# A decoder layer on one core: the operands that TensorE streams are put 64 bytes off the ones it keeps, and the MLP gets a fifth weight buffer

## Chip, cores and metric

One NeuronCore of a Trainium2 chip runs the whole layer as one program. The metric is the device time of one execution in microseconds; the time before is the median of 3 runs. TensorE (PE in the profile) multiplies, VectorE (DVE) and ScalarE (ACT) prepare operands and do the element-wise work, SyncE (SP) issues the DMAs that bring weights from HBM to SBUF. PEld is TensorE's loading of the operand that it keeps.

## What is computed

One layer over 16 meta tokens and 256 real tokens with model width 2048, in float32:

```
u = rmsnorm(h, g_mix);  proj = u @ w_in            # 2048 x 6144, q/k/v of both head groups
o_diff = rmsnorm(differential attention, 8 heads)  # softmax(q1 k1) - lam * softmax(q2 k2)
o_sb = rmsnorm(stick-breaking attention, 8 heads)
h = h + concat(o_diff, o_sb) @ w_out               # 2048 x 2048
m = rmsnorm(h, g_mlp)
h = h + square(relu(m @ w_up)) @ w_down            # 2048 x 8192 x 2048
return h without the meta tokens
```

## The kernel before

**Products in three.** Every float32 operand of a large matmul is kept as two tiles of TensorE's rounded float32 type: `hi`, a rounded copy made by ACT, and `lo`, the rest, made by DVE (`split`, lines 168 to 173). A product is then three matmuls: hi by hi, hi by lo and lo by hi. Each matmul has an operand that TensorE keeps (`lhsT`, 128 columns, loaded ahead) and one that it streams (`rhs`, 256, 272 or 512 columns).

**Parts.** Weights arrive by DMA in blocks of 128 x 1024 (`raw`, five buffers) and are split into a *part*: a `whi` and a `wlo` tile. There are 96 parts of `w_in`, 32 of `w_out` (numbers 96 to 127 here) and, from `first_mlp` on (number 128), those of the MLP. Three part buffers serve the first two stages. The MLP has four (`MLP_PARTS`): the fourth, tag "v", holds each part whose number counted from 128 leaves 3 when divided by 4. A part is prepared up to `MLP_LEAD` parts ahead of the one that TensorE uses, and a buffer is free again once the part `MLP_PARTS` back has been used (`ring`).

**Three stages.** (1) `w_in`, up to about 340 us: `products` (lines 944 to 956) keeps a block of weights and streams a row of `u`, 272 columns wide; for two of the six kinds of strips (`a in (0, 3)`, the queries) the first 16 columns, the meta tokens, are left out and 256 are streamed. Attention of finished heads is woven in between. (2) `w_out`, up to about 434 us: `triple` keeps `mixed` and streams 512 columns of weights. (3) The MLP in 8 rounds of 1024 hidden columns: `triple2` keeps `w_up` and streams 256 columns of `m` (line 1038), and `triple` keeps `hid` and streams `w_down` (line 1044). In three of the four column groups of rounds 0 to 6, and one in round 7 (`FAST`), a 2 x 2 block product is done with seven block products in place of eight; its seven weight blocks come from one load as part "a" (split of 768 columns, then three sums on DVE, lines 267 to 272, that turn `raw` into four further blocks) and part "b" (split of those). "b" can only be split once the sums of "a" are there. The other column groups are done plainly, 512 columns at a time.

**Order.** All instructions are recorded in a fixed order by a planner (`Pace`), which has a time estimate of its own for each engine and lets a job (a split, an evacuation) go into the queues when its inputs are due. On the chip each engine works through its queue strictly in that order. The evacuation of an up strip (`up_evac`, lines 841 to 870) makes `hx` and `hid` on ACT and DVE; the latter is what the down products of the next round keep.

**Where things lie.** The addresses in a partition are fixed when the program is built. Taken modulo 128 bytes: `u` (and `m`, in the same place), `mixed`, the `hid` of even rounds and the three part buffers all start at 32; the `hid` of odd rounds (a tile of its own) and the fourth part buffer start at 96. Parts, `m`, `mixed` and `hid` have rows of 1024 bytes or multiples of 512, so each block in them keeps its tile's remainder. A row of `u` has 272 columns, 1088 bytes, which is 8 x 128 + 64: its `hi` rows stand at 32 and its `lo` rows at 96. Where the 16 meta columns are left out, 64 bytes are added. The text below calls the start of the kept operand minus the start of the streamed one, modulo 128, the **offset** of a matmul. Before, it is 0 or 64 in all large matmuls:

| matmuls | streamed columns | count | offset before |
|---|---|---|---|
| up | 256 | 3072 | 0 in 2640 (110 parts), 64 in 432 (18 parts in the fourth buffer) |
| down, seven products | 256 | 1848 | 0 in 921, 64 in 927: even rounds 0 (fourth buffer 64), odd rounds 64 (fourth buffer 0) |
| down, plain | 512 | 480 | 0 in 240, 64 in 240 |
| out | 512 | 384 | 0 |
| in, keys and values | 272 | 1536 | in turn 0, 64, 0 within each product |
| in, queries | 256 | 768 | in turn 64, 0, 64 within each product |

The last 16 KB that the change uses come from a scratch area for DMA descriptors at the bottom of each partition, 16,384 bytes before (`dynamic_dma_scratch_size` at its default); the kernel issues all its DMAs from SP.

Of the kernel before, what the change touches and what calls it, by code (L numbers as in the profile page):

```python
# [7 lines left out]
F32 = mybir.dt.float32  # L8
F32R = mybir.dt.float32r
AF = mybir.ActivationFunctionType  # L10
ALU = mybir.AluOpType
AX = mybir.AxisListType

P = 128
DM = 2048
SEQ = 256
META = 16
TOK = META + SEQ
KT = DM // P
EPS = 1e-6  # L20
NEG = -1e30
ROUNDS = 8
PAIRS = 4
RAW = 5
# [1 line left out]
KINDS = ((0, 3, 1, 2, 4, 5), (1, 0, 2, 4, 3, 5), (1, 0, 2, 4, 3, 5), (1, 0, 4, 3, 2, 5))  # L26
PARTS = 3
LEAD = 2
MLP_PARTS = 4
MLP_LEAD = 3  # L30
FAST = {(r, u) for r in range(ROUNDS - 1) for u in range(3)} | {(ROUNDS - 1, 0)}
PSUM_BANKS = {"acc": 4, "att": 4}
SLOTS = {"k": 4, "q": 4, "v": 2, "e": 3, "pr": 2, "ah": 2, "m": 2, "n": 2}
# [86 lines left out]
def hymba_layer(ctx: ExitStack, tc: tile.TileContext, xT_d, xh_d, win_d, wout_d, wup_d, wdn_d, cst_d, par_d, out_d):  # L120
    nc = tc.nc
    cp = ctx.enter_context(tc.tile_pool(name="const", bufs=1))
    big = ctx.enter_context(tc.tile_pool(name="big", bufs=1))
    wp = ctx.enter_context(tc.tile_pool(name="weights", bufs=1))
# [10 lines left out]
    def as32(ap):  # L135
        return ap.bitcast(F32)
# [18 lines left out]
    cst = tp.tile([P, C_ID], F32, bufs=1, name="cst")  # L155
    ident = cp.tile([P, P], F32, name="ident")
    xT = big.tile([P, KT, TOK], F32, tag="x", name="xT")
    um = big.tile([P, KT, 2, TOK], F32R, tag="act", name="u")
    mixed = big.tile([P, KT, 2, SEQ], F32R, tag="mix", name="mixed")

    def split_u(k):
        g = par[:, G_MIX + k : G_MIX + k + 1]
        nc.scalar.activation(um[:, k, 0, :], xT[:, k, :], AF.Copy, scale=g)
        nc.vector.scalar_tensor_tensor(
            um[:, k, 1, :], xT[:, k, :], g, as32(um[:, k, 0, :]), op0=ALU.mult, op1=ALU.subtract
        )

    def split(hi, lo, src, n):
# [7 lines left out]
    strips = []  # L176
# [9 lines left out]
    order = [("in", *u) for u in dict.fromkeys(u[:2] for u in units)]  # L186
# [3 lines left out]
    def up(r, i, cs):  # L190
        return [("up", r, i, c) for c in cs if r < ROUNDS]

    def down(r, u, ps):
        return [(x, r, u, p) for p in ps for x in ("ab" if (r, u) in FAST else "a")]

    order += up(0, 0, range(3)) + up(0, 1, range(3)) + up(0, 0, (3,)) + up(0, 1, (3,)) + up(0, 2, range(4)) + up(0, 3, range(4))
    for r in range(ROUNDS - 1):
        c = iter([key for i in range(PAIRS) for key in up(r + 1, i, range(4))])
# [4 lines left out]
        assert not [*c, *d]  # L203
    ab = iter(down(ROUNDS - 1, 0, range(PAIRS)))
    d = iter([key for u in (1, 2, 3) for key in down(ROUNDS - 1, u, range(PAIRS))])
    order += [next({"d": d, "a": ab, "b": ab}[x]) for x in "dd" + "adbd" * 4 + "dd"]
# [5 lines left out]
    def source(g):  # L212
        what, *at = order[g]
        if what == "in":
            (_, a, b), c = strips[at[0]], at[1]
            return win_d[a, b][:, 4 * c : 4 * c + 4]
        return {"out": wout_d, "up": wup_d, "a": wdn_d}[what][tuple(at)]

    raws, parts, raw_at, done_at, parted = {}, {}, {}, {}, set()
    dma = [1700.0]  # L220

    def load(dst, src, n):
        nc.sync.dma_start(dst, src)
        dma[0] = max(dma[0], pc.pe + 1700) + n * 1.42
        return dma[0] + 400

    def fetch(number, pieces=1):
        if number < len(loads):
            g = loads[number]
            raws[g] = wp.tile([P, 4, 256], F32, tag="raw", bufs=RAW, name=f"raw_{g}")  # L230
            n = 4 // pieces
            for i in range(pieces):
                k = slice(n * i, n * i + n)
                raw_at[g, i] = load(raws[g][:, k], source(g)[:, k], n * 256)
                yield
# [3 lines left out]
    def part(g, pieces=1):  # L239
        if g < len(order) and g not in parts:  # L240
            pool, bufs, tag = wp, PARTS, "w"
            if g >= first_mlp:
                ring[g] = max(g - MLP_PARTS, first_mlp - PARTS + (g - first_mlp) % MLP_PARTS) if (g - first_mlp) % MLP_PARTS < PARTS else g - MLP_PARTS
                if (g - first_mlp) % MLP_PARTS >= PARTS:
                    pool, bufs, tag = mp, MLP_PARTS - PARTS, "v"
                    ring[g] = ring[g] if g - MLP_PARTS >= first_mlp else -1
            hi = pool.tile([P, 4, 256], F32R, tag=tag + "hi", bufs=bufs, name=f"whi_{g}")
            lo = pool.tile([P, 4, 256], F32R, tag=tag + "lo", bufs=bufs, name=f"wlo_{g}")
            parts[g] = (hi, lo)
            what, *at = order[g]  # L250
            fast = what in "ab" and (at[0], at[1]) in FAST
            pc.job("weights", (fast_a if what == "a" else fast_b)(g, hi, lo) if fast else halves(g, hi, lo, pieces))
# [31 lines left out]
    def halves(g, hi, lo, pieces):  # L284
        n = 4 // pieces
        for i in range(pieces):
            src = (g, i) if (g, i) in raw_at else (g, 0)
            while src not in raw_at or ring[g] >= 0 and ring[g] not in done_at:
                yield pc.pe + 200, None
            yield max(raw_at[src], done_at.get(ring[g], 0.0)), "a"  # L290
            k = slice(n * i, n * i + n)
            t = yield from split(hi[:, k], lo[:, k], raws[g][:, k], 256 * n)
            for kk in range(n * i, n * i + n):
                pc.at["w", g, kk] = t
        parted.add(g)
# [3 lines left out]
    g = 0  # L299
    for c in range(4):  # L300
        n = 2 if c == 0 else 4
        w = fetch(g, 4 // n) if g < RAW else None
# [473 lines left out]
    m = H = mp = None  # L776
# [52 lines left out]
    def mtile(tag, shape, name, bufs=1, dt=F32):  # L829
        return mp.tile(shape, dt, tag=tag, bufs=bufs, name=name)  # L830
# [2 lines left out]
    hid, Z = {}, {}  # L833

    def hidden(r):
        if r % 2:
            hid[r] = mtile("hid", [P, PAIRS, FULL, 2, P], f"hid_{r}", 1, F32R)
        else:
            hid[r] = big.tile([P, PAIRS, FULL, 2, P], F32R, tag="mix", name=f"hid_{r}")
# [32 lines left out]
    def plain_evac(r, u, o):  # L872
        yield from pc.until("R2")
        yield pc.pe, "v"
        for i in range(2):
# [3 lines left out]
            pc.give("acc", t)  # L879
            if r == ROUNDS - 1:  # L880
                nc.sync.dma_start(out_d[:, u, i], H[:, u, i])
# [86 lines left out]
    def later(number):  # L968
        while number < len(loads) and loads[number - RAW] not in parted:
            yield pc.pe + 200, None  # L970
        yield from ((pc.pe, None) for _ in fetch(number))
# [20 lines left out]
    for g in range(LEAD + 1):  # L992
        part(g, 2)
# [8 lines left out]
    def begin(g, lead):  # L1002

        if g:
            for later_g in range(g + 1, g + lead + 1):
                if later_g <= g + LEAD or later_g >= first_mlp:
                    part(later_g, 2 if later_g < 6 else 1)
        if g in load_of:
            pc.job("fetch", later(load_of[g] + LEAD + RAW))

    for s, c, kks in units:
        g = index["in", s, c]
# [6 lines left out]
        hi, lo = parts[g]  # L1019
        for j in range(2):  # L1020
            for kk in kks:
                k = 4 * c + kk
# [27 lines left out]
    for g in range(index["out", 0, 0], first_mlp):  # L1050
        _, u, c = order[g]
        if c == 0:
            out = banks("acc", 2, f"out_{u}")
            if u == 0:
                m = big.tile([P, KT, 2, SEQ], F32R, tag="act", name="m")
        if u == 1 and c == 0:
            while pc.lanes["head"][0] or any(("mixed", k) not in pc.at for k in range(KT)):
                pc.pe += 100
                pc.pump()
            attention.close()  # L1060
            mp = ctx.enter_context(tc.tile_pool(name="mlp", bufs=1))
        begin(g, LEAD)
        hi, lo = (x.rearrange("p (k a) b -> p k (a b)", k=2) for x in parts[g])
        for kk in range(2):
            k = 2 * c + kk
            pc.stall(("w", g, 2 * kk + 1), ("mixed", k))
            for i in range(2):
                x = [mixed[:, k, a, P * i : P * i + P] for a in range(2)]
                t = triple(out[i], x, (hi[:, kk], lo[:, kk]), k == 0, k == KT - 1)
                pc.pump()  # L1070
        done_at[g] = pc.pe
        if c == 7:
            pc.job("evac", after(t, out_evac(u, out)))
            if u == 3:
                pc.job("once", mlp_norm())

    for g in range(first_mlp, len(order)):
        what, r, u, p = order[g]
        begin(g, MLP_LEAD)
        hi, lo = parts[g]  # L1080
        pc.stall(("w", g, 3))
        if what == "up":
# [3 lines left out]
            for j in range(2):  # L1086
                for kk in range(4):
                    k = 2 * p + kk % 2 + 8 * (kk // 2)
                    pc.stall(("m", k))
                    w = [x[:, kk, P * j : P * j + P] for x in (hi, lo)]  # L1090
# [4 lines left out]
        else:  # L1095
            fast = (r, u) in FAST
            pc.stall(("hid", r, p))
            x = lambda slot: [hid[r][:, p, slot, a] for a in range(2)]
# [15 lines left out]
            else:  # L1114
                for i in range(2):
                    for k in range(2):
                        w = [y[:, 2 * k : 2 * k + 2].rearrange("p a b -> p (a b)") for y in (hi, lo)]
# [8 lines left out]
def _tables():  # L1126
# [12 lines left out]
    q, k = np.arange(P)[:, None], np.arange(P)[None, :]  # L1139
    cst[:, C_MD : C_MD + P] = np.where(k <= q, 0.0, NEG)  # L1140
    strict = np.where(k < q, 0.0, NEG)
    cst[:, C_MS + K0 : C_MS + TOK] = strict
# [44 lines left out]
```

## Time and profile before

| | |
|---|---|
| median of 3 runs | 1145.86 us (1145.79 to 1147.93) |
| the profiled execution | 1145.84 us, of which the span of instructions is 1144.0 us |
| busy: PE, PEld, DVE, ACT | 1131.5, 1082.5, 950.1, 799.2 us |
| granted clock of TensorE | 1.000 |
| HBM read | 206.49 MB |

Matmuls overlap in the records (each lasts about 0.28 us, and the next starts about 0.12 us after it), so that PE's busy time says little: its pace is read from the starts. In the chain of waits, a piece "PE up L1038 x24" is a run of 24 matmuls on the path that ends last, with its length in us ahead of it.

### The profile page before, as it was taken

The numbers are of one execution on the slowest core, as the hardware profiler recorded it, in microseconds if no ns is written. First come the engines' busy times: TensorE is split into PE (matmuls) and PEld (weight loads), VectorE is DVE, ScalarE is ACT, GpSimd is POOL, SyncE is SP. The second block draws the span as 40 slices with busy tenths as digits, with TensorE's granted clock in tenths as the row PEclk, the third lists the DMA queues.
The fourth block names the chain that finished last, engine by engine and source line by source line (L and its number), as shares of the span: only waits on it lengthen the run. The fifth ranks groups of instructions, "written<-read, shape, count | busy, mean of one in ns | idle before, by whom it ended". The sixth has DMA issues, their size and how long they took to land.

```text
span 1144.0 us, 21838 instructions
## 1 busy us (share of the span) xinstructions
PE 1131.5 (99%) x8599; PEld 1082.5 (95%) x8599; DVE 950.1 (83%) x1459; ACT 799.2 (70%) x1283; POOL 1.1 (0%) x8
## 2 busy tenths in 40 slices
PE   9999999999999999999999999999999999999998
PEld 7999999999998889999999999999999999999987
DVE  6987987887976556788888898898888888888997
ACT  7769888778776545666677676677677677677763
POOL 0000000000000000000000000000000000000000
PEclk9999999999999999999999999999999999999999
DMA  8564544555545556556555555555555655565554
GB/s 328 185 221 138 158 133 148 155 157 156 160 147 168 184 184 201 166 185 197 197 193 189 184 195 190 183 192 193 192 186 187 203 198 186 189 198 187 186 184 163
DMA packets 58134, 210.00 MB, mean 184 GB/s; under 512 B 6576, under 2 KB 6832, under 8 KB 57904
## 3 DMA queue, kind: packets, MB, share of 16 engines
q1 hardware_dynamic: 58032, 208.61, 55.9%
q8 instruction: 67, 1.10, 0.4%
q14 instruction: 35, 0.29, 0.1%
HBM read 206.49 MB, written 2.10 MB: 182 GB/s over the span
## 4 chain that ended last, share of the span: by engine, by line
PE 81%; DVE 15%; issue 2%; ACT 2%; DMA 1%; SPq 0%; DVEq 0%; ACTq 0%
PE up L1038 25%; PE down L1044 19%; PE acc L953 8%; DVE wlo L172 8%; PE acc L955 8%; PE acc L954 8%; PE out L1044 8%; DVE raw L268 2%; ACT whi L170 2%; DVE raw L270 1%; DVE raw L272 1%; DVE hid L869 1%; DVE hx L857 1%; PE s_d L603 1%; PE po_s L643 1%
## 5 line engine op out<-in xcount | busy, mean ns | idle before, releaser
L170 ACT CAST whi<-raw 128x1024 fp32r<-128x1024 f32 (+2 forms) x478 | 470.6, 997 | 277.1 <-PE up L1038 82.4
L172 DVE TENSOR_TENSOR wlo<-raw,whi 128x1024 fp32r<-128x1024 f32 (+2 forms) x478 | 543.9, 1158 | 137.3 <-ACT whi L170 133.0
L1038 PE MATMUL up<-m,whi 128*128 128x256 f32 x2048 | 369.9, 282 | 0.0
L1044 PE MATMUL down<-whi,hid 128*128 128x256 f32 (+1 forms) x1552 | 321.1, 303 | 0.0
L1038 PEld LDWEIGHTS up<-m,whi 128*128 128x128 f32 x2048 | 318.3, 191 | 1.8
L1038 PE MATMUL up<-m,wlo 128*128 128x256 f32 x1024 | 288.6, 282 | 0.0
L1044 PEld LDWEIGHTS down<-whi,hid 128*128 128x128 f32 x1552 | 247.7, 189 | 11.8 <-ACT down L905 0.2
L1044 PE MATMUL down<-wlo,hid 128*128 128x256 f32 (+1 forms) x776 | 238.2, 307 | 5.9 <-DVE wlo L172 4.5
L953 PE MATMUL acc<-u,whi 128*128 128x272 f32 (+1 forms) x768 | 223.6, 291 | 0.9 <-ACT whi L170 0.9
L955 PE MATMUL acc<-u,wlo 128*128 128x272 f32 (+1 forms) x768 | 220.2, 287 | 0.7 <-DVE wlo L172 0.7
L954 PE MATMUL acc<-u,whi 128*128 128x272 f32 (+1 forms) x768 | 219.7, 286 | 0.0
L1038 PEld LDWEIGHTS up<-m,wlo 128*128 128x128 f32 x1024 | 195.3, 191 | 0.0
L1044 PEld LDWEIGHTS down<-wlo,hid 128*128 128x128 f32 x776 | 146.6, 189 | 18.5 <-DVE wlo L172 12.0
L953 PEld LDWEIGHTS acc<-u,whi 128*128 128x128 f32 x768 | 144.8, 189 | 2.8 <-ACT whi L170 1.8
L955 PEld LDWEIGHTS acc<-u,wlo 128*128 128x128 f32 x768 | 144.7, 188 | 1.6 <-DVE wlo L172 1.5
L954 PEld LDWEIGHTS acc<-u,whi 128*128 128x128 f32 x768 | 145.1, 189 | 0.0
L1044 PE MATMUL out<-whi,mixed 128*128 128x512 f32 x256 | 79.9, 393 | 0.0
L268 DVE TENSOR_TENSOR raw<-raw 128x512 f32<-128x512 f32 x88 | 60.9, 692 | 3.0
L1044 PEld LDWEIGHTS out<-whi,mixed 128*128 128x128 f32 x256 | 47.2, 188 | 9.3
L1044 PE MATMUL out<-wlo,mixed 128*128 128x512 f32 x128 | 50.0, 390 | 0.0
L900 ACT COPY z<-down 128x512 f32<-128x512 f32 (+1 forms) x88 | 45.5, 528 | 0.1
L905 ACT COPY down<-z 128x512 f32<-128x512 f32 (+1 forms) x76 | 40.9, 538 | 2.4
(241 smaller groups left out, 896.3 us busy)
## 6 DMA issues: line engine op xcount, KB each, us to landing
raw<-in_wup SPq DMA_DIRECT2D x128, 512.0 KB, 4.5
raw<-in_wdn SPq DMA_DIRECT2D x128, 512.0 KB, 3.6
raw<-in_win SPq DMA_DIRECT2D x95, 512.0 KB, 3.7
raw<-in_wout SPq DMA_DIRECT2D x32, 512.0 KB, 3.5
H<-in_xh SPq DMA_DIRECT2D x1, 2048.0 KB, 8.3
out<-H SPq DMA_DIRECT2D x8, 256.0 KB, 2.0
xT<-in_x SPq DMA_DIRECT2D x3, 544.0 KB, 9.5
cst<-in_cst SPq DMA_DIRECT2D x1, 609.0 KB, 10.7
```

The costliest lines, as they stand in the source:

```text
L170: nc.scalar.copy(hi, src)
L172: nc.vector.tensor_tensor(lo, src, as32(hi), op=ALU.subtract)
L268: nc.vector.tensor_tensor(raw[:, 3::-3], first, raw[:, 3:1:-1], op=ALU.add)
L270: nc.vector.tensor_tensor(raw[:, 2], raw[:, 3], raw[:, 2], op=ALU.add)
L272: nc.vector.tensor_tensor(raw[:, 1], raw[:, 2], raw[:, 1], op=ALU.add)
L900: nc.scalar.copy(Z[u][:, at], o[i][:, :n])
L905: nc.scalar.copy(new[i][:, :n], Z[u2][:, at])
L953: nc.tensor.matmul(o, lhsT=h, rhs=xh, start=first, stop=False)
L954: nc.tensor.matmul(o, lhsT=h, rhs=xl, start=False, stop=False)
L955: nc.tensor.matmul(o, lhsT=l, rhs=xh, start=False, stop=last)
L1038: nc.tensor.matmul(out, lhsT=w[a], rhs=x[:, b], start=first and i == 0, stop=last and i == 2, skip_group_check=True)
L1044: nc.tensor.matmul(out, lhsT=x[a], rhs=w[b], start=first and i == 0, stop=last and i == 2, skip_group_check=check)
```

## The change

The tiles are moved by small pads so that the offset is 64 in every large matmul. The rows of `u` grow to 320 columns (1280 bytes, 10 x 128), so `hi` and `lo` rows have the same remainder. `u`, `m`, `mixed`, `hid` of all rounds start at 96; all part buffers start at 32 and are 1088 columns wide (4352 bytes, 34 x 128), and the parts of query strips are written 16 columns in, at 96, to match the 64 bytes that those strips are streamed later. The MLP has five part buffers (two of tag "v") and splits four parts ahead. The scratch area shrinks to 1024 bytes. The pads `pad_act` to `pad_mlp` are tiles that nothing uses.

```
+ROW = 320
+LINE = 16
-MLP_PARTS = 4
-MLP_LEAD = 3
+MLP_PARTS = 5
+MLP_LEAD = 4
+MLP_PAD = 1
...
-    um = big.tile([P, KT, 2, TOK], F32R, tag="act", name="u")
+    big.tile([P, LINE], F32, name="pad_act")
+    um = big.tile([P, KT, 2, ROW], F32R, tag="act", name="u")
+    big.tile([P, 2 * LINE], F32, name="pad_mix")
     mixed = big.tile([P, KT, 2, SEQ], F32R, tag="mix", name="mixed")
...
-        nc.scalar.activation(um[:, k, 0, :], xT[:, k, :], AF.Copy, scale=g)
+        nc.scalar.activation(um[:, k, 0, :TOK], xT[:, k, :], AF.Copy, scale=g)
...
+            if not raws:
+                wp.tile([P, LINE], F32, name="pad_w")
...
-            hi = pool.tile([P, 4, 256], F32R, tag=tag + "hi", bufs=bufs, name=f"whi_{g}")
-            lo = pool.tile([P, 4, 256], F32R, tag=tag + "lo", bufs=bufs, name=f"wlo_{g}")
+            shift = LINE if order[g][0] == "in" and strips[order[g][1]][1] in (0, 3) else 0
+            hi, lo = (
+                pool.tile([P, 1024 + 4 * LINE], F32R, tag=tag + x, bufs=bufs, name=f"w{x}_{g}")[:, shift : shift + 1024]
+                .rearrange("p (k n) -> p k n", k=4)
+                for x in ("hi", "lo")
+            )
...
+        if r == 1:
+            mp.tile([P, 3 * LINE], F32, name="pad_hid")
...
-                m = big.tile([P, KT, 2, SEQ], F32R, tag="act", name="m")
+                m = big.tile([P, KT, 2, ROW], F32R, tag="act", name="m")[:, :16].rearrange("p k a n -> p (k a n)")[:, : KT * 2 * SEQ].rearrange("p (k a n) -> p k a n", k=KT, a=2)
...
+            mp.tile([P, MLP_PAD * LINE], F32, name="pad_mlp")
...
-    nc = bacc.Bacc("TRN2", target_bir_lowering=False, num_devices=1)
+    nc = bacc.Bacc("TRN2", target_bir_lowering=False, num_devices=1, dynamic_dma_scratch_size=1024)
```

PE's own instructions stay in the same order, but for four transposes of the norm between the stages that move by a dozen places. The split work of the MLP moves a little on ACT, DVE and SP, because parts may now be prepared one further ahead. The first place is early in round 1 of the MLP, on DVE. `wlo_156` is the split of an "a" part, the three `raw_156` rows its sums, the three `hx_1_0` rows and `hid_1` the evacuation of the first up strip of round 1, `wlo_157` the "b" part that TensorE needs directly after 156. Before:

```order
L172 TENSOR_TENSOR wlo_156_6490<-raw_156_6354,whi_156_6489 128x768
L268 TENSOR_TENSOR raw_156_6354<-raw_156_6354 128x2x256
L270 TENSOR_TENSOR raw_156_6354<-raw_156_6354 128x256
L272 TENSOR_TENSOR raw_156_6354<-raw_156_6354 128x256
L857 TENSOR_TENSOR hx_1_0_6500<-hx_1_0_6500 128x2x128
L859 TENSOR_TENSOR hx_1_0_6500<-hx_1_0_6500 128x128
L861 TENSOR_TENSOR hx_1_0_6500<-hx_1_0_6500 128x128
L172 TENSOR_TENSOR wlo_158_6525<-raw_158_6430,whi_158_6524 128x1024
L172 TENSOR_TENSOR wlo_157_6506<-raw_156_6354,whi_157_6505 128x1024
L869 TENSOR_TENSOR hid_1_6553<-hx_1_0_6500,hid_1_6553 128x8x128
L172 TENSOR_TENSOR wlo_159_6563<-raw_159_6416,whi_159_6562 128x1024
```

And with the change, at the same place:

```order
L177 TENSOR_TENSOR wlo_156_6466<-raw_156_6341,whi_156_6465 128x768
L279 TENSOR_TENSOR raw_156_6341<-raw_156_6341 128x2x256
L281 TENSOR_TENSOR raw_156_6341<-raw_156_6341 128x256
L283 TENSOR_TENSOR raw_156_6341<-raw_156_6341 128x256
L870 TENSOR_TENSOR hx_1_0_6507<-hx_1_0_6507 128x2x128
L872 TENSOR_TENSOR hx_1_0_6507<-hx_1_0_6507 128x128
L874 TENSOR_TENSOR hx_1_0_6507<-hx_1_0_6507 128x128
L177 TENSOR_TENSOR wlo_158_6517<-raw_158_6423,whi_158_6516 128x1024
L177 TENSOR_TENSOR wlo_157_6503<-raw_156_6341,whi_157_6502 128x1024
L177 TENSOR_TENSOR wlo_159_6536<-raw_159_6410,whi_159_6535 128x1024
L882 TENSOR_TENSOR hid_1_6561<-hx_1_0_6507,hid_1_6561 128x8x128
```

The order up to `wlo_157` is the same; `hid_1` now stands behind one more split. What differs ahead of it is when the split of part 156 may start: its buffer is freed by part 151 now, and by part 152 before. The second place is the same step in round 3, on DVE, before:

```order
L861 TENSOR_TENSOR hx_3_1_8831<-hx_3_1_8831 128x128
L172 TENSOR_TENSOR wlo_257_8856<-raw_257_8741,whi_257_8855 128x1024
L172 TENSOR_TENSOR wlo_256_8837<-raw_255_8674,whi_256_8836 128x1024
L869 TENSOR_TENSOR hid_3_8622<-hx_3_1_8831,hid_3_8622 128x8x128
L172 TENSOR_TENSOR wlo_258_8893<-raw_258_8753,whi_258_8892 128x768
L268 TENSOR_TENSOR raw_258_8753<-raw_258_8753 128x2x256
```

And with the change:

```order
L874 TENSOR_TENSOR hx_3_1_8839<-hx_3_1_8839 128x128
L177 TENSOR_TENSOR wlo_257_8849<-raw_257_8739,whi_257_8848 128x1024
L177 TENSOR_TENSOR wlo_256_8835<-raw_255_8678,whi_256_8834 128x1024
L177 TENSOR_TENSOR wlo_258_8868<-raw_258_8752,whi_258_8867 128x768
L279 TENSOR_TENSOR raw_258_8752<-raw_258_8752 128x2x256
L281 TENSOR_TENSOR raw_258_8752<-raw_258_8752 128x256
L283 TENSOR_TENSOR raw_258_8752<-raw_258_8752 128x256
L882 TENSOR_TENSOR hid_3_8630<-hx_3_1_8839,hid_3_8630 128x8x128
```

Here `hid_3` moves behind the whole of an "a" part, four instructions.

More of the change, by code (lines that the diff above doesn't have):

```diff
@@ L162, in split_u @@
         g = par[:, G_MIX + k : G_MIX + k + 1]
-        nc.scalar.activation(um[:, k, 0, :], xT[:, k, :], AF.Copy, scale=g)
+        nc.scalar.activation(um[:, k, 0, :TOK], xT[:, k, :], AF.Copy, scale=g)
         nc.vector.scalar_tensor_tensor(
-            um[:, k, 1, :], xT[:, k, :], g, as32(um[:, k, 0, :]), op0=ALU.mult, op1=ALU.subtract
+            um[:, k, 1, :TOK], xT[:, k, :], g, as32(um[:, k, 0, :TOK]), op0=ALU.mult, op1=ALU.subtract
         )
```

## The prediction

> **What bounds the kernel now.** I read the page's head and the shares of the chain of waits first, to know whose time the span is.
>
> ```profile
> span 1144.0 us, 21838 instructions
> PE 1131.5 (99%) x8599; PEld 1082.5 (95%) x8599; DVE 950.1 (83%) x1459; ACT 799.2 (70%) x1283; POOL 1.1 (0%) x8
> PE 81%; DVE 15%; issue 2%; ACT 2%; DMA 1%; SPq 0%; DVEq 0%; ACTq 0%
> ```
>
> TensorE carries 81% of the path that ends last and DVE 15%. The sum below is made against the profiled execution, 1145.84 us (a span of 1144.0 us and 1.84 us around it), which is 0.02 us from the median of the three runs. What a measurement of this kernel can tell from no change is about 0.2%, 2.3 us.
>
> The change alters no matmul, only where operands lie. So the question is whether the pace of matmuls depends on that, and the trace of before can answer it, since offsets 0 and 64 both occur in it under otherwise equal matmuls. I went to the timeline of TensorE and took the starts of whole parts. The up matmuls first; one part is 24 of them. Part 155 (fourth buffer, offset 64) runs from the first row to the second, part 158 (an ordinary buffer, offset 0) from the third to the fourth.
>
> ```profile
> 501.50 0.39 PE L1038 MATMUL up<-m,whi 128*128 128x256 f32 x2
> 504.22 0.40 PE L1044 MATMUL down<-whi,hid 128*128 128x256 f32 x2
> ...
> 507.13 0.40 PE L1038 MATMUL up<-m,whi 128*128 128x256 f32 x2
> 510.01 0.64 PE L1044 MATMUL down<-whi,hid 128*128 128x512 f32 x2
> ```
>
> 2.72 us against 2.88 us, 113.3 against 120.0 ns a matmul. The buffer itself could be the reason, so the same is needed with the roles turned. The down products give it: the `hid` of odd rounds moves the offset by 64. Four parts "b" of 12 matmuls, each as its first row and the first row of the next part: 154 (round 0, ordinary buffer, offset 0), 187 (round 0, fourth, 64), 195 (round 1, fourth, 0), 198 (round 1, ordinary, 64).
>
> ```profile
> 500.06 0.40 PE L1044 MATMUL down<-whi,hid 128*128 128x256 f32 x2
> 501.50 0.39 PE L1038 MATMUL up<-m,whi 128*128 128x256 f32 x2
> ...
> 566.59 0.40 PE L1044 MATMUL down<-whi,hid 128*128 128x256 f32 x2
> 567.97 0.39 PE L1038 MATMUL up<-m,whi 128*128 128x256 f32 x2
> ...
> 582.80 0.40 PE L1044 MATMUL down<-whi,hid 128*128 128x256 f32 x2
> 584.24 0.40 PE L1038 MATMUL up<-m,whi 128*128 128x256 f32 x2
> ...
> 588.13 0.39 PE L1044 MATMUL down<-whi,hid 128*128 128x256 f32 x2
> 589.49 0.28 PE L1038 MATMUL up<-m,whi 128*128 128x256 f32 x1
> ```
>
> 1.44, 1.38, 1.44 and 1.36 us: 120, 115, 120 and 113 ns. The offset decides, not the buffer and not the round. This is the ground of the forecast: 256-column matmuls whose kept and streamed operands stand 64 bytes apart (modulo 128) follow each other 5 to 7 ns sooner.
>
> The Trainium skill speaks against it. Its page "SBUF — State Buffer", section "Who interferes with whom", says "PE and ACT never wait on anyone", and "TensorE: Matmul & The Clock Gate", Part 2, gives TensorE two independent read ports, so that loading the next kept operand takes nothing from the streaming one. By that rule the offset is worth nothing; the four parts above do not agree with it, since address alone separates 120 from 113 ns.
>
> **The change part by part.** The counts come from the groups of matmuls with shapes kept apart; a product has two matmuls with `whi` and one with `wlo`, or for the inputs one on each of three lines, so each group stands for 1.5 or 3 times its count.
>
> ```profile
> L1038 PE MATMUL up<-m,whi 128*128 128x256 f32 x2048 | 369.9, 282 | 0.0
> L1044 PE MATMUL down<-whi,hid 128*128 128x256 f32 x1232 | 222.1, 280 | 0.0
> L953 PE MATMUL acc<-u,whi 128*128 128x272 f32 x512 | 150.9, 295 | 0.0
> L1044 PE MATMUL down<-whi,hid 128*128 128x512 f32 x320 | 99.4, 392 | 0.0
> L1044 PE MATMUL out<-whi,mixed 128*128 128x512 f32 x256 | 79.9, 393 | 0.0
> L953 PE MATMUL acc<-u,whi 128*128 128x256 f32 x256 | 72.7, 284 | 0.9 <-ACT whi L170 0.9
> ```
>
> *Up.* Of 2048 x 1.5 = 3072 matmuls, 2640 have offset 0. Each gains 120.0 - 113.3 = 6.7 ns: 17.7 us.
>
> *Down, 256 columns.* Of 1848, 921 have offset 0. 120 less the mean of 115 and 113.3 is about 5.9 ns: 5.4 us.
>
> *In.* Here the offset alternates within a product, and no stretch has it at 64 throughout. The pace of the alternating pattern is read from a run of queries (81 matmuls from the first row to the second, 80 steps) and one of keys or values (19 steps):
>
> ```profile
> 298.72 0.28 PE L953 MATMUL acc<-u,whi 128*128 128x256 f32 x1
> 308.22 0.28 PE L955 MATMUL acc<-u,wlo 128*128 128x256 f32 x1
> ...
> 223.48 0.29 PE L954 MATMUL acc<-u,whi 128*128 128x272 f32 x1
> 225.86 0.29 PE L955 MATMUL acc<-u,wlo 128*128 128x272 f32 x1
> ```
>
> 9.50/80 = 118.8 ns and 2.38/19 = 125.3 ns. So two matmuls of three at 64 hardly help the queries, as if one load at the wrong distance spoilt its neighbours. At 64 throughout, the nearest row is the up part at 113.3 ns for the same 256 columns: 768 x 5.5 ns = 4.2 us. For 272 columns no row has the good pattern. The bounds are 0 (it stays at 125.3) and the 6.7 ns of the up matmuls, so 0 to 10.3 us for 1536 matmuls; I take the queries' 5.5 ns, the row from the same stage and pattern, 8.4 us.
>
> *512 columns.* Offset 0 is a run of `out`, offset 64 a down part of round 1:
>
> ```profile
> 374.52 18.42 PE out L1044 x81
> ...
> 570.99 2.75 PE down L1044 x12
> ```
>
> 18.42/81 = 227.4 and 2.75/12 = 229 ns. No gain, rather 1.5 ns lost on the 384 of `out` and the 240 of down that change: +0.9 us. Bounds: 0 and +2 us.
>
> Matmuls together: 17.7 + 5.4 + 4.2 + 8.4 - 0.9 = 34.8 us.
>
> *The fifth buffer.* TensorE still waits for DVE in the MLP, and the chain shows why:
>
> ```profile
> PEld down L1044 <- DVE wlo L172: 12.0, 29, 0.7
> ...
> 496.28 2.76 PE up L1038 x23
> 499.06 0.84 ACT whi L170
> ...
> 499.92 0.97 DVE wlo L172
> ...
> 500.92 0.70 DVE raw L268
> ...
> 503.43 2.36 DVE wlo L172 x2
> ...
> 505.84 1.45 PE down L1044 x10
> ```
>
> Part 156 is split only when TensorE has finished 152 (499.04), because that part holds its buffer; then DVE needs 6.8 us in one line, split, three sums, three `hx` steps and the splits of 158 and 157, and TensorE is there at 505.3. With five buffers part 151 frees the place at about 496.1. The split and sums, 0.97 + 0.70 + about 0.9 us, then lie ahead of the `hx` steps, which wait for the up strip anyway; 157 is ready some 2 us earlier, more than the longest wait of 0.7 us. That pays if DVE has room, see below. Of the 12.0 us I take 8 as saved (bounds 0 and 12), since a faster TensorE also reaches each part sooner. The later `hid` costs nothing: it is kept by products of the next round. The DMAs are the same in number; some swap places by one on SP's queue. Five `raw` buffers for parts four ahead leave about two in flight, and TensorE needs a load in 2 to 3 us: enough, with landings around 4 us. The smaller scratch area: all DMAs are SP's, I cost it at nothing. Wider rows of `u` and parts: same elements, nothing.
>
> *What loses its cover.* DVE and ACT have the same work in less time.
>
> ```profile
> core 0: us, PE busy (x) PEld busy (x) DVE busy (x) ACT busy (x) POOL busy (x), PEclk, DMA share, GB/s
> 33.00:130.00 97.00, 97.00 (x794) 96.13 (x793) 85.80 (x185) 79.58 (x177) 0.00 (x0) 1.00 0.55 175
> 501.50:589.50 88.00, 87.36 (x687) 84.52 (x686) 76.32 (x99) 57.72 (x73) 0.00 (x0) 1.00 0.59 192
> 1029.90:1102.00 72.10, 71.55 (x541) 68.28 (x540) 66.53 (x95) 51.24 (x67) 0.00 (x0) 1.00 0.59 194
> ```
>
> A round of the MLP (second row) would take about 88.0 - 3.0 (330 up at 6.7 ns, some 126 down at 5.9) - 1.2 of waits = 83.8 us: DVE 76.32/83.8 = 91%. The third row shows DVE at 66.53/72.10 = 92% while TensorE goes on, so there is room, barely. Yet in the end of that stretch DVE is the chain:
>
> ```profile
> 1087.72 2.09 DVE wlo L172 x2
> ...
> 1092.77 4.31 DVE wlo L172 x4
> ```
>
> There the gain of matmuls does not shorten the path; from 1077 to 1112 that is about 5% of 35 us, +2 us. In the first row DVE goes from 88% to 85.8/92.6 = 93%, while attention's small matmuls in TensorE's strict order wait for DVE's results: +4 us for the first stage (bounds 0 and 8).
>
> Sum: 1145.84 - 34.8 - 8 + 2 + 4 = 1109.0 us.
>
> **The rivals.**
>
> *Keys and values stay at 125 ns.* A 272-column row is longer than the others and might fall out of step. For it: 512 columns show no gain. Against it: 272 is close to 256, and 512 is not. The 8.4 us stay: 1117 us.
>
> *DVE becomes the pace in the MLP.* For it: the 15% of the chain, the pieces at 1087 to 1097, and 91% in a strict queue that also waits for ACT. Then a round stays at its 88 us and no waits are saved: 6 rounds x 3.0 and 2 for the last, 20 us, and the 8 come back: 1137 us. Against it: 92% was run in the third row, and the split starts a part earlier. From a DVE share of about 93% this would decide.
>
> *Reads that do not meet.* If kept and streamed operands are read without regard to each other, the 7 ns belong to something that the parts share by chance, and only the buffer helps: 1145.84 - 8 = 1138 us. The Trainium skill's rule on the ports (above) is this rival's. Four combinations of buffer and round speak against it.
>
> *The change does not do what it says.* With the reads as in that rival and a split that starts no earlier because DVE is not free, 1146 us.
>
> *Slower: `hid` too late.* The evacuations now stand behind up to four split instructions (an "a" part, about 2.6 us) on DVE. If TensorE waited for each of the 28 evacuations of rounds 1 to 7, 28 x 2.6 = 73 us would come on top: 1145.84 - 35 + 73 = 1184 us; it exceeds the gain from 1.5 us of wait each. Against it: `hid` of the last up strip of a round is first kept by the fourth down part of the next, some 16 us later by the parts of the timeline above, and the wait list names `wlo`, never `hid`.
>
> **How the numbers follow.** Forecast, offsets and buffer as worked out: 0.72. Keys and values without gain 0.08, DVE as the pace 0.13, reads that do not meet 0.03, no effect 0.02, `hid` too late 0.02. Predicted is the forecast's 1109 us. Around it lie 4 us up or down for the first stage, 8 up or 4 down for the waits and 8 up or 2 down for 272 columns; not all at once. I take 1101 to 1126 us, which holds the forecast but for a small part, the first rival, and milder forms of the second, about 8 in 10. Faster by over 0.2%: 0.72 + 0.08 + 0.13 + 0.03 = 0.96; within 0.2%: 0.02; slower: 0.02.
>
> **What would show it.** Right: up parts of 24 at 2.72 us in every buffer, all 12-matmul "b" parts near 1.36 us, 272-column starts 120 ns apart, 512-column ones at 227 to 230; waits of PEld for `wlo` in the MLP below 5 us; DVE's time unchanged at about 950 us and its share near 86%. Wrong: up parts at 2.88 us in all buffers (the distance is not what counts), 272 at 125 ns, or rounds of 88 us with long waits for `wlo` (DVE), for `hid`, or for `raw` (the loads).

## The result, and the profile after

The changed kernel takes 1132.22 us (median of 4 runs, 1132.04 to 1132.49) against 1146.89 us for the kernel before on the same chip (4 runs, 1145.79 to 1148.19): a ratio of 0.987, 95% interval 0.986 to 0.989. It is faster, by 1.3%, and 23 us slower than the 1109.0 us forecast, outside the range.

The head of the page after, and the shares of its chain of waits:

```profile
span 1130.7 us, 21822 instructions
...
PE 1124.5 (99%) x8599; PEld 1081.4 (96%) x8599; DVE 946.8 (84%) x1459; ACT 798.3 (71%) x1283; POOL 1.1 (0%) x8
...
PE 98%; DVE 1%; ACT 0%; DMA 0%; issue 0%; SPq 0%; ACTq 0%
```

DVE's 15% of the path is now 1%. In the list of waits (engine and line, what it waited for: us in all, times, longest) TensorE's 12.0 us for `wlo` in the down products are gone; what is left of its waits for splits and evacuations is small:

```profile
PEld acc L966 <- ACT whi L175: 1.3, 1, 1.3
...
PEld down L1057 <- ACT down L918: 0.9, 1, 0.9
...
PEld acc L968 <- DVE wlo L177: 0.6, 3, 0.2
```

The chain in the middle of the MLP (start us, length us, what) is TensorE alone, where that of before went through DVE again and again (in the prediction's rows from 499 to 505 us):

```profile
599.68 2.82 PE up L1051 x24
602.51 2.47 PE down L1057 x21
604.98 2.83 PE up L1051 x24
```

An up part of 24 takes 2.83 us, 117.8 ns a matmul, in every buffer: neither the 2.88 us of offset 0 nor the 2.72 us forecast. The down products of 21 go at the same pace. Two of the stretches of the prediction, in the first stage and in the MLP, and one run of `out`:

```profile
33.00:130.00 97.00, 97.00 (x791) 96.21 (x789) 85.47 (x182) 79.11 (x176) 0.00 (x0) 1.00 0.55 175
501.50:589.50 88.00, 88.00 (x704) 85.97 (x703) 78.01 (x102) 59.57 (x76) 0.00 (x0) 1.00 0.58 196
```

```profile
398.71 18.56 PE out L1057 x81
```

The MLP's 88 us hold 704 matmuls instead of 687, the first stage's 97 us 791 instead of 794. The clock is 1.00 in both traces. The 81 matmuls of `out` take 18.56 us, 229 ns each, where they took 18.42.

Adding up the steps from each matmul's start to the next, by group (a step counts with the matmul it starts from), gives where the 13.3 us of span came from. A wait is a step more than 25 ns above the group's median; its excess over the mean pace is counted as waiting:

| matmuls | before: us, pace, waits | after: us, pace, waits |
|---|---|---|
| up | 365.2, 118.8 ns, 0.2 | 361.9, 117.8 ns, 0.2 |
| down, 256 columns | 229.7, 117.1 ns, 13.3 | 218.5, 117.8 ns, 0.9 |
| in, 272 columns | 196.7, 125.4 ns, 4.2 | 198.4, 126.5 ns, 4.2 |
| in, 256 columns | 94.4, 118.5 ns, 3.4 | 94.0, 117.5 ns, 3.8 |
| down, 512 columns | 110.6, 229.6 ns | 110.1, 229.8 ns |
| out | 88.3, 227.9 ns | 88.8, 229.2 ns |

Waits of the down products give 12.4 us of it. All paces together (up -3.3, down +1.1, in +1.7 and -0.8 us) give another 1.3 us, where 34.8 were forecast.

### The profile page after: what moved, and what is told of

Read it like the earlier page. It is cut to its first block, busy times and chain, and to the rows that moved or that the text cites. A ratio compares the mean times of both kernels' runs of the same rounds, so it can differ in the third digit from the quotient of the medians.

```text
span 1130.7 us, 21822 instructions
## 1 busy us (share of the span) xinstructions
PE 1124.5 (99%) x8599; PEld 1081.4 (96%) x8599; DVE 946.8 (84%) x1459; ACT 798.3 (71%) x1283; POOL 1.1 (0%) x8
## 4 chain that ended last, share of the span: by engine, by line
PE 98%; DVE 1%; ACT 0%; DMA 0%; issue 0%; SPq 0%; ACTq 0%
PE up L1051 32%; PE down L1057 28%; PE acc L966 9%; PE acc L968 9%; PE acc L967 8%; PE out L1057 8%; PE s_d L614 1%; PE po_s L654 1%; PE po_d L654 1%; PE z_s L614 1%; PE pt L818 0%; DVE wlo L177 0%; ACT whi L175 0%; DMA xT<-in_x 0%; PE pq_dq L542 0%; PE pv_s L591 0%
## 5 line engine op out<-in xcount | busy, mean ns | idle before, releaser
L175 ACT CAST whi<-raw 128x1024 fp32r<-128x1024 f32 (+2 forms) x478 | 465.6, 997 | 217.9 <-PE up L1051 61.0
L1051 PEld LDWEIGHTS up<-m,whi 128*128 128x128 f32 x2048 | 314.2, 188 | 1.9
L1057 PEld LDWEIGHTS down<-whi,hid 128*128 128x128 f32 x1552 | 246.6, 188 | 12.3 <-ACT down L918 0.9
L1057 PE MATMUL down<-wlo,hid 128*128 128x256 f32 (+1 forms) x776 | 234.9, 303 | 0.0
L1051 PEld LDWEIGHTS up<-m,wlo 128*128 128x128 f32 x1024 | 191.9, 187 | 0.0
L862 ACT ACTIVATE hx<-up 128x512 f32<-128x512 f32 x32 | 19.1, 597 | 44.1 <-PE up L1051 44.1
```

Source lines behind the costliest of these rows:

```text
L175: nc.scalar.copy(hi, src)
L862: nc.scalar.activation(x[:, 0:4].rearrange("p a b -> p (a b)"), o, AF.Relu)
L1051: nc.tensor.matmul(out, lhsT=w[a], rhs=x[:, b], start=first and i == 0, stop=last and i == 2, skip_group_check=True)
L1057: nc.tensor.matmul(out, lhsT=x[a], rhs=w[b], start=first and i == 0, stop=last and i == 2, skip_group_check=check)
```

## The experiments

**The two halves, and the pace by itself.** Four kernels ran on one chip. Their texts compare theory L, that what ran ahead decides between 113.3 and 117.8 ns at the same offset, with A, that the place in SBUF decides, and B, that TensorE cannot be fed any faster for long.

`five_alone`: the kernel before with the fifth buffer.

```
-MLP_PARTS = 4
-MLP_LEAD = 3
+MLP_PARTS = 5
+MLP_LEAD = 4
...
+... dynamic_dma_scratch_size=1024)
```

> The kernel before with five part buffers, four parts ahead and the small scratch area; no operand is moved on purpose (two of five buffers start at 96 now, so 1152 up matmuls have offset 64 where 432 had). Theory L (a lock: at offset 64 the pace is either 113.3 ns or 117.8 ns, and which one is kept from what ran before): the waits of the down products for DVE, 12.4 us by the starts, go as they did with the whole change, and the up parts at 64 run at 113.3 ns since parts at 0 stand between them: 1146 - 12 - 4 = 1130 us, not slower than the whole change. Rival A (the place of tiles in SBUF, not the history, makes 117.8): the same, 1130 us, as the tiles stay near their old places. Rival B (TensorE's instructions are handed out at no more than one pair in 117.8 ns on average): 1133 us, since parts at 113.3 must be paid back.

`offset_alone`: the changed kernel with `MLP_PARTS = 4`, `MLP_LEAD = 3`.

> The whole change but with four part buffers and three parts ahead. All theories: the pace stays at 117.8 ns, and the waits for DVE come back: matmul pace gives 1 to 2 us by the starts of the changed kernel, so 1143 to 1146 us.

Measured: `five_alone` 1130.88 us, ratio to before 0.987 (0.985 to 0.988); `offset_alone` 1144.96 us, 0.999 (0.998 to 1.000). The buffer alone is the whole gain, the offsets alone are worth nothing that can be told. The chain of `five_alone` and TensorE's waits in `offset_alone`:

```profile
PE 97%; DMA 2%; ACT 1%; SPq 0%; DVE 0%; issue 0%; ACTq 0%
```

```profile
PEld down L1057 <- DVE wlo L177: 12.3, 30, 0.7
PE down L1057 <- DVE wlo L177: 4.6, 16, 0.4
```

With four buffers the waits stay at 12.3 us although every offset is 64; with five they go although most offsets are 0. Of the 109 stretches at 64 bytes in up and down of `five_alone`, 66 were quick (113 to 115 ns) and 43 slow (117 ns or more), although runs at 0 stand between them, which theory L had taken to be enough.

`one_zero`: the changed kernel, with the parts of one buffer in five moved by 64 bytes, so that their offset is 0.

```
-... in (0, 3) else 0
+... in (0, 3) or g >= first_mlp and (g - first_mlp) % MLP_PARTS == 4 else 0
```

> The whole change, but the MLP parts of one of the five buffers are written 64 bytes further, so that their matmuls have offset 0. Theory L: matmuls at 0 bring the two reads into the step from which 113.3 ns follows; the other four buffers run at 113.3, this one at 120: mean 114.6 in place of 117.8 ns for 4920 matmuls, 16 us less, 1117 us. Rival A: 117.8 and 120 ns, 1134 us. Rival B: no mean below 117.8, 1132 us.

1133.20 us, ratio 0.989 (0.987 to 0.990). Runs at offset 0 do not bring the quick pace back (177 of 182 stretches at 64 in up and down stay slow):

```profile
604.51 2.87 PE up L1051 x24
607.38 2.47 PE down L1057 x21
609.85 2.83 PE up L1051 x24
```

The first row is at offset 0 (2.87 us), and the parts behind it stay at 2.47 and 2.83 us. That part of L, that a run at 0 helps the next one at 64, fell.

`offsets`: matmuls of two fixed tiles, without the layer.

```
+ for n in (256, 272, 512):
+     for st, mv in ((0, 0), (16, 0), ..., (64, 0), ..., (0, 64), (64, 64)):
+         wait(); run(36, n, st, mv)
+         wait(); run(24, 256, 0, 0); run(36, n, st, mv)
...
+ run(24, 256, 0, 0); run(400, 256, 64, 0)
```

> A kernel of its own that leaves the layer out: runs of equal matmuls on two tiles with nothing else going on, at offsets 0 to 112 by 16 bytes and with 256, 272 and 512 columns, each once after a wait and once straight after 24 matmuls at offset 0; then 24 at 64, a few at 0 and 36 at 64; then 400 at 64. Theory L: at 64 the run after a wait is at 117 to 118 ns, the run after offset 0 at 113; a few matmuls at 0 suffice to change over; 400 in a row stay at 113. Rival A: both runs at 64 have the same pace. Rival B: a run begins at 113 and falls to 117.8 within some dozens of matmuls. For 272 columns I expect 120 ns in the good state and 126 otherwise.

Two windows of 3.80 us, both of 256 columns, kept operand at 64 and streamed at 0 bytes, the same tiles; the first run follows a wait, the second a run at offset 0 (PE's count is in the first bracket):

```profile
74.60:78.40 3.80, 3.80 (x36) 3.80 (x35) 0.00 (x0) 0.00 (x0) 0.00 (x0) 1.00 0.02 4
82.50:86.30 3.80, 3.80 (x34) 3.80 (x33) 0.00 (x0) 0.00 (x0) 0.00 (x0) 1.00 0.00 0
```

By starts, the first settles at 113.3 ns and the second at 117.8, from its first matmul to its last; the 400 stay at 117.8 throughout. So the offset of 64 has two steady paces, and L had their order the wrong way round. Place (A) cannot be the reason, as the tiles are the same. B does not hold: the second takes 117.8 ns from its first matmul, and 60 matmuls at 64 bytes behind twelve of 512 columns (from 623.59 us) kept 113.2 ns to their end. One matmul at offset 0 was enough to change over, but from quick to slow: behind 1 to 12 of them, all seven runs took 117.8 ns, and six of the seven had run at 113.3 ahead of them. Offsets other than 0 and 64 gave 117 to 123 ns. 272 columns took 125.2 ns at offset 0 and 123.3 at 64 with the kept operand on the later side, 126.7 with the streamed one there; 512 columns 226.7 at offset 0 and 229 to 233 at 64.

**Which side.** In the changed kernel up has its kept operand at 32 and its streamed one at 96 bytes ("streamed later" below), down the reverse ("kept later"). Three kernels vary that; the offset stays 64 everywhere.

`same_side`: kept at 96 in `out`, up and down.

```
-... in (0, 3) else 0
+... in (0, 3) or order[g][0] == "up" else 0
-... name="m")...[:, : KT * 2 * SEQ]
+... name="m")...[:, LINE : LINE + KT * 2 * SEQ]
```

> The changed kernel with m moved on by 16 elements and the up parts shifted by 16, so that through out and the whole MLP the kept operand starts 96 bytes and the streamed one 32 bytes past a multiple of 128 (in the changed kernel the up matmuls have kept 32, streamed 96; keys and values too, and they stay so). The distance stays 64 bytes everywhere. Theory S (which of the two stands on the later 64 bytes decides, and the quick pace of 113.3 ns needs the kept one there): the 4920 matmuls of 256 columns of up and down go from 117.8 to 113.3 ns, 22 us; 1110 us if waits don't grow. Theory T (only history decides, whatever stands where): the arrangement in up and down changes nothing; 117.8 ns stays, 1132 us.

1129.60 us, ratio 0.986 (0.984 to 0.987). `same_side_in` adds the same for keys and values (`u` and its parts moved by 64 bytes).

> As the kernel with one side in the MLP, and also u at 32 and the parts of keys and values at 96, so that the 272-column matmuls have kept 96, streamed 32. (The queries go the other way round: kept 32, streamed 96.) Theory S: 1536 matmuls of 272 columns at about 123.3 instead of 126.5 ns, 5 us more: 1105 us; queries stay near 117 ns. Theory T: 1132 us.

1128.90 us, 0.985 (0.984 to 0.987); 272 columns stayed at 126.4 ns. `other_side`: kept at 32, streamed at 96 in up and down.

```
+... or order[g][0] in "ab" else 0
-mixed = big.tile([P, KT, 2, SEQ], ...)
+mixed = big.tile([P, KT * 2 * SEQ + LINE], ...)[:, : KT * 2 * SEQ]...
-hid[r] = mtile("hid", [P, PAIRS, FULL, 2, P], ...)
+hid[r] = mtile("hid", [P, PAIRS * FULL * 2 * P + LINE], ...)[:, LINE : ...]
...
-wp.tile([P, LINE], F32, name="pad_w")
+wp.tile([P, 2 * LINE], F32, name="pad_w")
```

> The changed kernel with hid moved on by 16 elements and the down parts shifted by 16, so that in the MLP every kept operand starts at 32 and every streamed one at 96 bytes. Theory S: no matmul has the quick arrangement, up and down stay at 117.8 ns, 1132 us; 512-column down products perhaps some ns off. Theory T: the arrangement is uniform as in the kernel with one side, so both give the same time, be it 1110 or 1132 us.

1121.71 us, 0.979 (0.978 to 0.980): theory S had it the wrong way round, and T, that the two sides are equal, fell too. The chain of `same_side` behind a 512-column part, and that of `other_side`:

```profile
596.11 2.77 PE down L1057 x12
598.87 2.72 PE up L1051 x24
601.59 2.48 PE down L1057 x21
604.07 2.83 PE up L1051 x24
```

```profile
484.10 2.48 PE down L1057 x21
486.57 2.74 PE up L1051 x24
489.32 2.48 PE down L1057 x21
491.79 2.74 PE up L1051 x24
```

Up matmuls with the same remainders take 2.72 us in the first part and 2.83 in the next. So a step between up and down can change the pace where the side stays the same: in `same_side` from a quick up part to a slow down part at all 21 such steps. In `same_side` 28 of 199 stretches of up or down were quick (over 8 matmuls, judged by the mean of the last eight), in `other_side` 71, in the changed kernel 1 of 199. Even the first stage sped up in `other_side`, although its tiles only moved by 128 bytes, parts and loads alike, and `u` not at all:

```profile
33.00:130.00 97.00, 96.46 (x801) 95.36 (x800) 86.59 (x187) 80.54 (x179) 0.00 (x0) 1.00 0.57 178
```

801 matmuls against 791 in the same 97 us; 272 columns at 123.6 ns instead of 126.5. So the remainder modulo 128 alone does not fix the pace there.

Modulo 256 bytes the rows come apart, which the runs were not made for but show. Kept minus streamed, modulo 256, is 192 in every large matmul of the changed kernel and of `same_side`. In `other_side` and `both_sides` (below) it is 64 in the first stage, in `out` and in up; in down it is 64 in even rounds and 192 in odd ones, because the `hid` of odd rounds is a tile of its own that moved 128 bytes further. The fixed tiles start alike modulo 256, so that the two sides are 64 (kept later) and 192 there. By their starts:

| matmuls | at 64 | at 192 |
|---|---|---|
| in, 272 columns (at 64 `other_side` and `both_sides`, at 192 the others with one distance) | 123.6 ns | 126.4 to 126.5 ns |
| 272 columns, fixed tiles (`offsets`) | 123.2 to 123.4 ns | 126.6 to 126.8 ns |
| out, 512 columns | 233.3 ns | 229.2 ns |
| 512 columns, fixed tiles (starts at 0 and 64 or 32 and 96) | 233.4 ns | 228.9 to 229.3 ns, once 233.4 |
| in, 256 columns (also `same_side_in` at 64) | 114.7 to 115.6 ns | 117.2 to 117.5 ns |

So the "offset 64" of this document holds two distances, and for 272 and 512 columns the pace follows which one it is, but for that one run. With 256 columns either one has shown 113.3 and 117.8 ns. But here, too, the rounds of `other_side` differ: of the 14 up parts between the down products of a round, 13 were quick in each even round (the rows of 484 to 494 us) and 1 in each odd one, rounds 0 to 6:

```profile
574.34 2.48 PE down L1057 x21
576.81 2.83 PE up L1051 x24
579.64 2.48 PE down L1057 x21
582.11 2.83 PE up L1051 x24
```

`sides`: fixed tiles again, in changing order.

```
+ A, B = (64, 0), (0, 64)        # kept, streamed
+ for what in (A, B): 8 x (wait(); run(30, 256, *what))
+ for first, then in ((A, B), (B, A)): 4 x (wait(); 4 x (run(24, first); run(12, then)); run(24, first))
```

> Leaves the whole layer out: matmuls of two fixed tiles alone, runs of chosen offsets (bytes past a multiple of 128 of kept and streamed operand), with and without a wait ahead. Theory S: (kept 64, streamed 0) after a wait runs at 113.3 ns every time, (0, 64) at 117.8 every time; a run of (0, 64) turns a following run of (64, 0) to 117.8. Theory T: both give 113.3 or 117.8 by what ran ahead, and their alternation changes nothing. By either, moving both operands on by the same bytes within 64 leaves the pace.

After a wait, A ran at 113.3 ns in seven of eight tries, B at 117.8 in eight of eight. One each (30 matmuls), A quick, A slow, B:

```profile
26.12 3.58 PE L36 MATMUL bank<-M,W 128*128 128x256 f32 x30
30.55 3.70 PE L36 MATMUL bank<-M,W 128*128 128x256 f32 x30
57.29 3.70 PE L36 MATMUL bank<-M,W 128*128 128x256 f32 x30
```

Alternation showed a rule that no expectation held: a step from A to B keeps the pace, a step from B to A changes it, from 113.3 to 117.8 and from 117.8 to 113.3, at each of the 32 steps of either kind, apart from the first matmuls of a run. B therefore also runs at 113.3 ns when it comes after a quick A, and in this part it did so behind three of four waits, too. S fell here as well. Twelve matmuls of 512 columns behind a slow A made the next A quick (113.4 ns), one left it slow (117.9). Moving both operands on by the same 16 to 48 bytes, once each behind a wait, gave 113.2 to 118.3 ns in no order; A itself took 117.9 this time.

**What sets it.** `reset`: `same_side`, with the up parts of one buffer in five left at 32 (offset 0).

```
-... or order[g][0] == "up" else 0
+... or order[g][0] == "up" and (g - first_mlp) % MLP_PARTS < 4 else 0
```

> The kernel with one side, but the up parts of one buffer in five are not shifted, so that kept and streamed operand both stand at 32 bytes there (576 of 3072 up matmuls at offset 0); all others of out and the MLP stay at kept 96, streamed 32. Theory R (a run at offset 0 puts the matmuls behind it into the quick state when it stands at 32 bytes, as it did for 60 of 62 such runs in the kernel before, and not when it stands at 96, as in the kernel with one buffer at offset 0): behind each such part the pace is 113.3 ns. If it then lasts, up 2496 matmuls and down 1848 gain about 4.5 ns on most: some 1113 us. If the next change of part ends it, as behind the 512-column parts in the kernel with one side, only some 20 parts of about 21 matmuls gain, 2 us, and the 576 at offset 0 lose 1.3 us: 1128 us. Theory H (the state at entry rules and nothing in the MLP sets it): 117.8 ns throughout but for the zero parts, 1131 to 1133 us.

1131.38 us, 0.988 (0.986 to 0.989), the time of theory H. The first row is such a part; what follows in 256 columns stays slow, at all 18 such places:

```profile
604.47 2.85 PE up L1051 x24
607.32 2.48 PE down L1057 x21
609.80 2.83 PE up L1051 x24
```

Modulo 256 these parts stand 128 bytes from what they stream, those of the kernel before 0 bytes, so that R was not put to the test at the distance that it was read from.

`zeros`: 24 fixed matmuls at offset 0, standing at 0, 32, 64 or 96 bytes, then runs at 64.

```
+ for z in (0, 32, 64, 96): for what in (A, B):
+     4 x (wait(); run(24, 256, z, z); run(36, 256, z + what[0], z + what[1]))
+     wait(); up(24, z, z); 3 x (down(24, z + what); up(24, z + what))
```

> Leaves the layer out: matmuls of fixed tiles alone. 24 matmuls of 256 columns at offset 0 standing at 0, 32, 64 or 96 bytes, then 36 at offset 64 to either side, four times each; then the same with the kernel's own order of operands (up: one kept operand twice, then another; down: one streamed operand twice, then another), changing between the two. Theory R: behind zeros at 32 bytes 113.3 ns, at 96 bytes 117.8 ns (0: 117.8, as measured). Theory H: 117.8 ns behind all zeros. If the order of operands matters, the state flips at a change from up to down.

Behind zeros at 0 and at 32 all 16 runs took 117.8 ns, behind zeros at 64 and at 96 all but one of 16 took 113.3. Theory R had it reversed, and H fell. In the kernel before nearly all runs behind zeros at 32 were quick (60 of 62 in the text of `reset`), so that what holds for these tiles does not carry over to the layer. The last line stands for both orders, up first and down first. With the kernel's order of operands, starts 2.82 us apart behind zeros at 32 and 2.72 behind zeros at 96, without a flip between the two orders (kept 96, streamed 32 in both):

```profile
365.49 2.99 PE L50 MATMUL side<-M,W 128*128 128x256 f32 x24
368.31 2.99 PE L50 MATMUL bank<-M,W 128*128 128x256 f32 x24
371.14 2.99 PE L50 MATMUL side<-M,W 128*128 128x256 f32 x24
...
572.96 2.88 PE L50 MATMUL bank<-M,W 128*128 128x256 f32 x24
575.68 2.88 PE L50 MATMUL side<-M,W 128*128 128x256 f32 x24
578.40 2.88 PE L50 MATMUL bank<-M,W 128*128 128x256 f32 x24
```

`both_sides`: `other_side` with `m` and the up parts moved as in `same_side`, so that up has kept 96, streamed 32 and down the reverse.

> The fourth arrangement: in the MLP the up matmuls have kept 96, streamed 32 and the down matmuls kept 32, streamed 96 (the changed kernel has the reverse of both; the two kernels with one side have one of them throughout). Distance 64 everywhere. Theory M (the rule of the runs of matmuls alone: a step from streamed-later to kept-later flips the pace, the other step keeps it): every second pair of up and down parts runs at 113.3 ns, 4920 x 4.5 / 2 = 11 us, 1121 us. Theory K (in the kernel something else rules, since the changed kernel's 77 steps of the flipping kind left 117.8 ns): down stays at 117.8 ns as in all three other arrangements, up quick in none to half of its parts, 1125 to 1132 us.

1118.65 us, ratio 0.976 (0.974 to 0.978), the fastest of all. Up and down gained 10.2 us on the changed kernel, by their starts, where theory M had 11; the first stage gained 5.7 more and `out` lost 1.5:

```profile
592.69 2.75 PE up L1051 x24
595.44 2.38 PE down L1057 x21
597.82 2.83 PE up L1051 x24
600.65 2.48 PE down L1057 x21
603.12 2.73 PE up L1051 x24
605.86 2.38 PE down L1057 x21
608.24 2.83 PE up L1051 x24
```

102 of 199 stretches are quick, for down too (2.38 us). That the whole lies below M's 1121 us is due to the first stage, of which M says nothing. At all 83 steps from down (streamed later) to up (kept later) the pace flips, 53 to quick and 30 to slow, as the rule of `sides` says. At the 77 steps from up to down it should stay; it did at 45: at all 33 in odd rounds, whose down products are at 192 modulo 256, and at 12 of 44 in even rounds, where they are at 64 like up. In the changed kernel, where the roles are exchanged modulo 128, it stayed at all 83 steps from down to up, as the rule says, but also at all 77 from up to down, where the rule has it flip. Read modulo 256 that is no exception, since up and down are both at 192 there and the distance never changes. The rule read so fails elsewhere, though: in the even rounds of `both_sides` the pace flips without a change of distance, and in the odd rounds of `other_side` it flipped at 6 of 36 steps from 192 to 64. What sets the pace of 256 columns in the layer is not settled.

## Why the prediction was wrong, step by step

*The fifth buffer: right, undersized.* The mechanism held: the split starts a part earlier, and DVE no longer sets the path, but for some 10 us of DVE and ACT near 1080 us that cost TensorE 0.9 us of waiting. 8 us were forecast, 12.4 came, just past the upper bound of 12. I had held back 4 us because a faster TensorE would reach each part sooner; it did not get faster.

*What loses its cover: not seen.* The +2 us at the end and +4 us in the first stage rested on a faster TensorE. DVE's share of the round is 78.01/88.0 = 89%, and waits in the first stage stayed at 4.2 us for 272 columns.

*Up: the step that failed.* "Each gains 120.0 - 113.3 = 6.7 ns: 17.7 us" took 113.3 ns for the pace of offset 64. It is one of two paces of that offset. Up gained 3.3 us, since its 432 matmuls that were quick before became slower while 2640 gained about 2 ns each. *Down* took the same step: 1.1 us lost instead of 5.4 gained.

"The offset decides, not the buffer and not the round" was read from four parts. By their starts 81 of the 94 stretches at offset 64 in the trace of before were quick and 13 slow, one of them at 615 us behind a wait. In the stretch at 592 us the steps are 113 to 114 ns up to a wait for DVE and, two steps on, 117 to 118. I had the trace to see it. And every stretch of 64 there lay between runs at 0, the longest with 66 matmuls, so that the trace held no example of what the change makes: 64 throughout.

*In: failed by the same step.* 272 columns went from 125.4 to 126.5 ns, 1.7 us lost where 8.4 were forecast, below the lower bound of 0 that I had set; the queries gained 0.8 us of 4.2. Even the better distance modulo 256, 123.6 ns, would have been worth 2.7 us. *512 columns* came within 1 us, as forecast. That the kernel got faster, as forecast, is the buffer's doing, the smaller term; the larger one gave 1.3 of its 34.8 us.

*The rivals.* "Reads that do not meet" has nearly the right outcome, only the buffer helps, but not its reason: addresses do matter, in `offsets` by 120.0 against 113.3 ns. The Trainium skill's rule behind that rival ("SBUF — State Buffer", "Who interferes with whom") is not borne out by these runs either; whether it is the two reads that meet was not shown. The Trainium skill's page "TensorE: Matmul & The Clock Gate", "Back-to-back issue gap", gives N/2.4 + 2.5 ns for an isolated matmul, an estimate of 109.2 ns for 256 columns; no pace that lasted here was below 113. "DVE becomes the pace" did not happen even in `both_sides`, which puts 714 matmuls into the 88 us.

Account, from 1109.0 us: paces 33.5 us short of their 34.8, the buffer 4.4 more, the 6 us of lost cover not spent: 1109.0 + 33.5 - 4.4 - 6 = 1132.1 us.

## What to carry over

A pace read from short stretches between other work need not be the pace of the same work in a row: before a term is multiplied by thousands, look for every stretch of that kind in the trace, those that took longer above all, and for one as long as the change would make. Take a wait that the chain names more seriously than a pace that seems to differ; one more buffer was the whole gain. Where two paces hang on what stands next to what, try all arrangements and time the whole kernel: five with the same offset and five buffers spanned 1118.7 to 1132.2 us. And a remainder is a choice of the one who tabulates: modulo 128 two distances looked alike that modulo 256 are 3 ns apart for 272 columns and 4 for 512.

## What the runs showed of the hardware

- TensorE's float32-rounded matmuls of 256 columns, each with a new kept operand, ran at 120.0 ns in fixed tiles with both operands at the same remainder modulo 128 bytes. With 64 bytes between them they settled at 113.3 or 117.8 ns; the slow pace lasted 400 in a row (`offsets`), the quick one 144 (`zeros`). A wait, another width or a change of side changed it in some cases and left it in others.
- 272 columns: 125.0 to 125.4 ns at the same remainder (`offsets`); with kept minus streamed at 64 modulo 256, 123.2 to 123.6 ns, at 192, 126.4 to 126.8, in kernels and fixed tiles alike. 512 columns in `out`: 227.9 ns at 0, 229.2 at 192, 233.3 at 64; here equal is best. In fixed tiles they took 226.7 ns at 0 and mostly 228 to 234 at 64 bytes; 226.7 came back in two of them, with the kept operand at 16 or 48 bytes (`sides`).
- In fixed tiles, moving from streamed-later to kept-later flips the pace and the way back keeps it; runs at the same remainder set it slow at 0 and 32 bytes and quick at 64 and 96, where a wait on matmuls at 0 came ahead. In the layer neither held throughout.
